# First token parts made from the loads in single steps, first casts shared with Pool, forget gate moved behind the third pair

## The chip, the cores and the metric

The kernel runs on one core of one Trainium2 chip. The metric is the device time of one execution in microseconds (us). Before the change it is 517.13 us, the median of 3 runs (516.63 to 520.16). Five engines work side by side, each through its own queue in order: TensorE (matmuls, transposes), VectorE, ScalarE, Pool (GpSimd) and SP, which here only issues DMAs. The profile calls them PE (its weight loads PEld), DVE, ACT, POOL and SP.

## What is computed

Two residual layers over 512 tokens of 1024 channels, everything in float32. Cut to what matters here, the first layer is:

```python
h = rms_norm(x, norm_g)
proj = h @ w_in
fox_qkv, f_logit, moba_qkv, gate = split(proj)          # 8 fox heads, 8 moba heads of 64
logf = log_sigmoid(f_logit + b_f)                       # one forget value per token and fox head
c = cumsum(logf)                                        # over tokens
logits = q @ k * scale + c[query] - c[key]              # fox: causal, biased by c
out_a = softmax(logits) @ v
out_b = moba(qb, kb, vb)                                # rotary, selected key blocks
x = x + (concat(out_a, out_b) * silu(gate)) @ w_out
```

The second layer is a GLU, a causal depthwise convolution of width 31, a layer norm and an output projection.

## The kernel before

A float32 product is made of three products of rounded parts: each operand is split into `hi` (rounded) and `lo` (the rest), and `hi*hi + hi*lo + lo*hi` is summed. So each block of weights (a chunk of 256 or 260 columns, 1024 rows, 1 MB) is loaded into `wst`, cast to `whi` by ScalarE (L237) and subtracted to `wlo` by VectorE or Pool (L241), in four pieces of 512 columns per partition. Two `wst` buffers let one chunk load while another is split.

**The start.** The tokens arrive transposed, `xt`, in four tiles of 128 tokens (8 channel blocks of 128 each, `fetch_xt`, L279). SP issues in this order: the first `xt` tile in two halves, the first weight chunk in four quarters, the other three `xt` tiles whole, then the untransposed `xs` tiles and the next chunk (L316 to L324). For each tile and half tile, VectorE multiplies by the norm's gain into `hn` (L409), ScalarE casts `hn` to `hhi` (L411), VectorE subtracts to `hlo` (L412). The first chunk's split stands behind the first tile's parts: ScalarE casts all four pieces, Pool subtracts the first and the third, VectorE the others. TensorE begins with 22 matmuls on zeros (`WARM`, L394) and then multiplies tile by tile, 24 matmuls for each (`tok_mm`, L442); for the first chunk all eight `hi*hi` come first, then eight `lo*hi`, then eight with `wlo`. The norm's own factor `rinv` per token comes from ScalarE's squares of `xs` (L419) and a power on Pool (L422), and is applied when a product is read out of PSUM (`qk_chunk`: L468, L470). The second chunk's split (ScalarE, VectorE) is queued behind the first two of these reads.

**The middle.** 16 chunks of projections (`dense`) are interleaved on TensorE with 8 pairs of attention heads (`attention`): pairs 0 to 3 are `moba`, 4 to 7 `fox`. A pair's tile (`tile_of`, L585) is two score matmuls (L590, L592) into one of two `s` banks, a VectorE step that adds the mask or bias and takes the row minimum (`p`, `nm`, L602), ScalarE's exponential (L603), transposes on TensorE into one of two `tp` banks (L606), and a copy out of that bank to `pt`, by ScalarE (L614) and VectorE (L616) in turn. `stacks` (L554) makes a pair's `q`, `k` and `kl` (L570 to L581). L683 multiplies with the values; the result is scaled by `rb`, which comes back from a DMA through `sdram` (L626, L629).

**The forget gate.** The seventh chunk holds the gate's 8 columns. When its last tile is read, `forget` (L513) runs: two VectorE steps on 32 columns, an exponential (L519), twelve more small VectorE steps (a series for the logarithm), a triangle of ones `tri` (an iota on Pool, a comparison on VectorE, L534), four matmuls in eight passes for the cumulative sum (L537), a copy `ct` and a DMA to `cdram` (L541). The fox pairs load their bias rows `cb` from there (L662), and Pool adds the mask to each (L598).

Beside this, Pool splits the weights of the last layer into DRAM (`presplit`, L712): a load by SP, a cast (L718), a subtraction (L719), two DMA issues (L721), for 16 parts.

**What sets the order.** `ORDER` (L79) holds, for each engine, the whole order of this part's instructions, written out as indices into the program; `+n` are steps of `presplit`. Every queue follows it to the letter, so a step that waits holds up everything behind it on its engine.

Of the kernel before, what the change touches and what calls it, by code (L numbers as in the profile page):

```python
# [66 lines left out]
def XLO(t, nc):  # L67
# [22 lines left out]
        694 857-858 788-789 779-782 859-868 721-722 869 817-818 749-750 870-877 851-852 878-880  # L90
        893-906 785-787 890 907-912 790-792 891 913-916 920-937 917 938-939 819-821 944-945 853-855
        822 918 856 940-941 847-850 942-943 948-956 972 881 973 892 1080-1081 957-966 882-888 919
        889 967-968 946-947 969 1085-1086 1114-1115 970-971 976-985 974-975 986-988 1082-1084
        989-990 1144-1145 991-1004 1087 1005 1088 1006 1089 1007-1023 1116-1119 1024-1034 1146-1149
        1035-1044 1072-1075 1174 1045-1056 1175-1182 1057-1071 1090-1113 1120-1143 1150-1173
        1189-1198 1076-1079 1199-1212 1219-1236 1183 1237-1242 1184 1248-1271 1213 1243-1244
        1277-1286 1301 1214 1302-1304 1185-1188 1287-1300 1313-1318 1272-1273 1319-1320 1309-1310
        1321-1322 1215-1218 1323-1328 1245-1247 1329-1335 1337-1338 1336 1344-1346 1305-1307
        1341-1342 1308 1347-1351 1274 1311 1275 1312 1276 1352-1356 1368-1369 1357-1367 1371-1384
        1339-1340 1385-1393 1404 1394 1343 1405 1410-1425 1370 1426-1429 1434 1430-1433 1464-1465  # L100
        1440 1395 1441-1443 1522 1435 1523-1525 1444-1445 1396-1403 1406-1409 1446-1451 1493-1494
        1530-1531 1436-1439 1452-1462 1466-1468 1463 1469-1476 1558-1559 1477 1586-1587 1478-1480
        1495-1497 1481-1482 1532-1533 1483-1492 1498 1613-1614 1499-1506 1560-1561 1507-1508 1588
        1509-1513 1526-1529 1514-1521 1534-1537 1615-1616 1538-1548 1625 1549-1551 1626 1552-1555
        1617-1622 1655 1623-1624 1719 1656 1720-1722 1556-1557 1685-1686 1627-1630 1562-1578
        1690-1691 1579-1580 1657-1660 1581-1584 1727-1728 1585 1687-1689 1723-1726 1589-1592
        1731-1732 1593-1595 1692-1694 1596-1599 1735-1736 1600-1612 1729-1730 1631-1632 1738-1739
        1633-1636 1733-1734 1750-1751 1637-1646 1737 1647-1648 1756-1757 1649-1653 1740 1654
        1661-1664 1762-1763 1665-1668 1741 1669-1673 1767-1768 1674-1675 1742-1747 1772-1773
        1748-1749 1752-1753 1758-1761 1754-1755 1676 1776-1777 1677-1684 1695-1705 1780-1781 1764  # L110
        1769 1783-1784 1770 1765 1771 1766 1706-1718 1774-1775 1778-1779 1782 1785-1797""",
    "DVE": """0 2 12 35-38 1 3 13 15 4-11 14 16-17 19 21 18 20 23 25 22 27 24 29 26 31 28 32 30 43-44
        39-42 33-34 45-47 49 51 50 52-53 48 54 65-66 83-84 55-56 58 85 59 89 57 92-94 96-98 60 95 99
        61-62 100 63 67 70 101 68 102 74 64 111-112 71 75 77 103 69 78 72 76 73 82 79 86 88 80 104
        122-123 90 124-125 105 108 87 109 126 113 91 106 114 81 107 110 118 129 119 121 115 130 137
# [41 lines left out]
WARM2 = 2  # L157
# [7 lines left out]
def tile_kernel(ctx: ExitStack, tc: tile.TileContext, x, xt, w, small0, small1, l1_norm, out):  # L165
# [59 lines left out]
    def split_w(w, ring, eng, parts, cast, swap):  # L225
# [559 lines left out]
    for tl in range(64):  # L785
        with tc.high_priority(HP):
            next(att)
# [522 lines left out]
```

## Time and profile before

| | |
|---|---|
| median of 3 runs | 517.13 us |
| the profiled execution | 519.09 us, of it 517.3 the span that the profile covers |
| busy in the span | TensorE 97%, VectorE 73%, ScalarE 62%, Pool 54% |
| granted TensorE clock, mean | 0.997 of full speed |
| DMA moved | 87.46 MB, mean 169 GB/s |

Times in the profile count from the span's start. A row of a timeline gives the start, the time from the first instruction's start to the last one's end, engine, line, operation, output and inputs, shapes and count, and in brackets the engine's idle time ahead with what ended it. Instructions of an engine overlap a little, so `x4` of 0.62 us can take 2.19 us in all. A DMA's row is its issue alone. A view of stretches gives each engine's busy time in a window, then the granted clock, the mean busy share of the 16 DMA engines and GB/s.

### The profile page before, as it was taken

How to read it: one execution, taken by the hardware profiler on the slowest of the kernel's cores; microseconds unless marked ns; L12 is line 12 of the kernel's file. 1: busy time of each engine (PE TensorE's matmuls, PEld its weight loads, DVE VectorE, ACT ScalarE, POOL GpSimd, SP SyncE). 2: the span in 40 equal slices, each digit the busy share in tenths (PEclk: the TensorE clock that was granted, in tenths of full speed). 3: DMA queues.
4: the chain of work that ended last, by engine and by line, in shares of the span. 5: the costliest groups of instructions: out<-in, count | busy, mean ns of one | idle time of the engine just before them, and what ended most of it. 6: DMA issues, size and time to landing. Idle time of an engine off the chain costs nothing.

```text
span 517.3 us, 9873 instructions
## 1 busy us (share of the span) xinstructions
PE 503.3 (97%) x3694; PEld 460.1 (89%) x3694; DVE 377.4 (73%) x790; ACT 322.3 (62%) x665; POOL 281.7 (54%) x315
## 2 busy tenths in 40 slices
PE   8999999997999999999999999999999999989997
PEld 4999998985889998878779999999999988868997
DVE  6744677779565677767688144999999999897741
ACT  5945678775545787556575723988878656567330
POOL 4265858277598454311402011787999997876200
PEclk9999999999999999999999999999999999989999
DMA  8842244657645450323207698588999947741111
GB/s 287 328 145 72 96 142 164 205 186 236 213 167 178 146 163 26 125 96 123 102 2 293 205 208 241 178 210 208 291 255 236 331 167 264 182 124 41 41 43 42
DMA packets 20856, 87.46 MB, mean 169 GB/s; under 512 B 2692, under 2 KB 5056, under 8 KB 13512
## 3 DMA queue, kind: packets, MB, share of 16 engines
q1 hardware_dynamic: 15512, 59.47, 32.3%
q0 software_dynamic: 5152, 27.27, 20.3%
q8 instruction: 29, 0.48, 0.4%
q14 instruction: 19, 0.16, 0.1%
q10 hardware_dynamic: 144, 0.09, 0.1%
HBM read 57.41 MB, written 10.53 MB: 131 GB/s over the span
## 4 chain that ended last, share of the span: by engine, by line
PE 82%; DVE 7%; DMA 4%; POOL 2%; issue 2%; ACT 2%; SPq 1%; POOLq 0%; ACTq 0%; DVEq 0%
PE mm L442 29%; PE mm L451 8%; PE mm L452 8%; PE mm L453 8%; PE st L442 4%; PE tp L606 3%; PE o L683 3%; PE st L451 2%; PE st L453 2%; PE st L452 2%; PE o L442 2%; PE s L590 2%; PE s L592 2%; POOL pacc L898 2%; DMA xt<-in_xt_dram 1%
## 5 line engine op out<-in xcount | busy, mean ns | idle before, releaser
L898 POOL TENSOR_TENSOR pacc<-pacc,tm 128x256 f32<-128x256 f32 (+1 forms) x129 | 125.2, 981 | 19.7 <-ACT tm L897 12.5
L888 DVE SCALAR_TENSOR_TENSOR s<-u,parts,s 128x256 f32<-128x256 f32 (+1 forms) x207 | 105.9, 566 | 0.7
L442 PE MATMUL mm<-whi,hhi 128*128 128x256 f32 (+1 forms) x352 | 99.0, 288 | 0.6 <-ACT whi L237 0.6
L442 PE MATMUL mm<-wlo,hhi 128*128 128x256 f32 (+1 forms) x352 | 98.7, 287 | 0.5 <-DVE wlo L241 0.4
L442 PE MATMUL mm<-whi,hlo 128*128 128x256 f32 (+1 forms) x352 | 98.3, 286 | 0.0
L897 ACT ACTIVATE tm<-u,parts 128x256 f32<-128x256 f32 (+1 forms) x129 | 69.0, 577 | 15.2 <-POOL pacc L898 14.8
L442 PEld LDWEIGHTS mm<-whi,hhi 128*128 128x128 f32 x352 | 65.8, 189 | 1.8 <-ACT whi L237 1.2
L442 PEld LDWEIGHTS mm<-wlo,hhi 128*128 128x128 f32 x352 | 65.8, 190 | 1.7 <-DVE wlo L241 0.6
L442 PEld LDWEIGHTS mm<-whi,hlo 128*128 128x128 f32 x352 | 65.8, 190 | 0.2
L237 ACT ACTIVATE whi<-wst 128x512 fp32r<-128x512 f32 (+2 forms) x77 | 49.4, 708 | 7.8 <-DMA wst<-in_w_dram 4.1
L603 ACT ACTIVATE p<-p,nm 128x128 f32<-128x128 f32 (+3 forms) x64 | 35.7, 559 | 26.1 <-DVE nm L602 24.2
L241 DVE TENSOR_TENSOR wlo<-wst,whi 128x512 fp32r<-128x512 f32 (+1 forms) x50 | 40.9, 848 | 10.5 <-ACT whi L237 10.3
L241 POOL TENSOR_TENSOR wlo<-wst,whi 128x512 fp32r<-128x512 f32 (+1 forms) x22 | 30.6, 1400 | 28.2 <-ACT whi L237 28.2
L598 POOL TENSOR_TENSOR cb<-cb,mask 128x128 f32<-128x128 f32 x32 | 16.9, 534 | 50.7 <-DVE nm L602 37.4
L451 PE MATMUL mm<-nhi,wx 128*128 128x256 f32 (+1 forms) x104 | 32.6, 313 | 0.0
L452 PE MATMUL mm<-nlo,whi 128*128 128x256 f32 (+1 forms) x104 | 31.9, 308 | 0.0
L452 PE MATMUL mm<-nlo,wx 128*128 128x256 f32 (+1 forms) x104 | 31.8, 306 | 0.0
L453 PE MATMUL mm<-nhi,wx 128*128 128x256 f32 (+1 forms) x104 | 31.8, 306 | 0.0
L453 PE MATMUL mm<-nhi,wlo 128*128 128x256 f32 (+1 forms) x104 | 31.8, 306 | 0.0
L451 PE MATMUL mm<-nhi,whi 128*128 128x256 f32 (+1 forms) x104 | 31.7, 307 | 0.0
L606 PE MATMUL tp<-identf,p 128*128 128x128 f32 x160 | 28.3, 274 | 0.4 <-ACT pt L614 0.3
L477 POOL TENSOR_TENSOR rq<-vq,mhalf 128x16 f32<-128x16 f32 x8 | 25.9, 3240 | 3.4 <-DVE vq L475 3.1
(295 smaller groups left out, 1475.1 us busy)
## 6 DMA issues: line engine op xcount, KB each, us to landing
wst<-in_w_dram SPq DMA_DIRECT2D x29, 1024.0 KB, 5.2
wx<-wst POOLq DMA_DIRECT2D x9, 1024.0 KB, 7.0
wlo<-wst POOLq DMA_DIRECT2D x7, 1024.0 KB, 9.3
pre<-ot POOLq DMA_DIRECT2D x26, 256.0 KB, 3.3
wx<-pre SPq DMA_DIRECT2D x4, 1024.0 KB, 5.2
ot<-in_w_dram SPq DMA_DIRECT2D x13, 256.0 KB, 5.6
wst<-in_w_dram SPq DMA_DIRECT2D x2, 1040.0 KB, 7.2
xs<-in_x_dram SPq DMA_DIRECT2D x4, 512.0 KB, 11.4
```

The source lines that it names most:

```text
L237: A.activation(hi[:, ks], st[:, ks], AF.Copy)
L241: (V if eng is G and parts == 4 and (k % 4 > 0) != swap else eng).tensor_tensor(lo[:, ks], st[:, ks], hi[:, ks].bitcast(F32), op=ALU.subtract)
L442: T.matmul(po, a[:, k, ts], b[:, k, :n], start=first and i == 0, stop=last and i == len(prods) - 1)
L451: T.matmul(po, whi[:, k, cs], a, start=k == 0, stop=False)
L452: T.matmul(po, whi[:, k, cs], b, start=False, stop=False)
L453: T.matmul(po, wlo[:, k, cs], a, start=False, stop=k == KC - 1)
L477: G.tensor_tensor(r, v, mhalf[:, :16].rearrange("p (t h) -> p t h", t=NT), op=ALU.pow)
L603: A.activation(p[:, :w], p[:, :w], AF.Exp, bias=nm, scale=-1.0, accum_out=sm[:, h, t:t + 1])
L606: T.transpose(tp[:, j * P:(j + 1) * P], p[:, j * P:(j + 1) * P], identf)
L888: V.scalar_tensor_tensor(acc[:, o], v, w, first[0][:, :n] if i == 1 else acc[:, o], op0=ALU.mult, op1=ALU.add)
L897: A.activation(tm[:, :n], v, AF.Copy, scale=w)
L898: G.tensor_tensor(pacc[:, o], pacc[:, o], tm[:, :n], op=ALU.add)
```

## The change

- The first `xt` tile is loaded whole, the first weight chunk in two halves.
- `hn` is gone. For each of the eight channel blocks of a tile, ScalarE makes `hhi` straight from `xt` with the gain as its scale, and VectorE makes `hlo` as `xt * gain - hhi` in one step. 8 casts and 8 subtractions of 512 columns become 32 and 32 of 128.
- Of the first chunk's casts, ScalarE does the first and third piece, Pool (`tensor_copy`) the second and fourth. All four subtractions are VectorE's. In Pool's order the two casts and two of the four `rinv` powers now stand ahead of the rope tables (L351, L355).
- `forget` is called after tile 26 of the attention (`FT`), inside the fourth pair. Its 14 small VectorE steps stand together, behind the two score reads that ran at 132.69 and 132.97 us before, and ahead of the tile copy of 136.14 (L616); its exponential on ScalarE behind the tile copy of 137.15 (L614); its matmuls on TensorE ahead of a product that ran at 145.55. `tri` is made on Pool (a memset and a select) in the buffer of tag `e`, behind the eleventh part of `presplit` and ahead of the weight subtraction of 140.33. On VectorE the product with `rb` of 115.84 (L688) moves behind a tile copy and a weight subtraction.
- On SP the gate's DMA stands behind a weight load, the two loads of the first `cb` behind the fourth pair's `sdram` and `rb`; on Pool the first two mask additions, which ran at 146.29, behind the weight subtraction of 161.05.
- TensorE's order is otherwise the same.

The diff without the lists of `ORDER`:

```diff
...
@@ -149,6 +148,7 @@
 L34 = (35,)
 POS7 = 0
 SP3 = 23
+FT = 26
 GLO = ()
 KO = 4
 KORD = (6, 0, 1, 2, 4, 5, 7, 3)
@@ -222,7 +222,13 @@
             SY.dma_start(st[:, k:k + m, :].rearrange("p k n -> p (k n)"), w_ap(off, n, k, m))
         return st, n
 
-    def split_w(w, ring, eng, parts, cast, swap):
+    def low_eng(i, j, eng, parts):
+
+        if eng is not G or parts != 4:
+            return eng
+        return V if i == 0 or (j % 2 == 1) != (i == V1) else G
+
+    def split_w(i, w, ring, eng, parts, cast):
         st, n = w
         if ring == "main":
             hi, lo = flat(main, F32R, "whi", n, 2), flat(main, F32R, "wlo", n, 2)
@@ -231,14 +237,17 @@
         m = KC // parts
         if cast:
             G.dma_start(hi, st)
-        for k in range(0, KC, m):
+        for j, k in enumerate(range(0, KC, m)):
             ks = slice(k, k + m)
-            if not cast:
+            if i == 0 and j % 2:
+                G.tensor_copy(hi[:, ks], st[:, ks])
+            elif not cast:
                 A.activation(hi[:, ks], st[:, ks], AF.Copy)
             if eng is None:
                 A.activation(lo[:, ks], st[:, ks], AF.Copy, scale=-1.0)
             else:
-                (V if eng is G and parts == 4 and (k % 4 > 0) != swap else eng).tensor_tensor(lo[:, ks], st[:, ks], hi[:, ks].bitcast(F32), op=ALU.subtract)
+                low_eng(i, j, eng, parts).tensor_tensor(lo[:, ks], st[:, ks], hi[:, ks].bitcast(F32),
+                                                        op=ALU.subtract)
         if eng is None:
             G.dma_start(lo.bitcast(F32), st, accum_op=ALU.add)
         return hi, lo
@@ -290,7 +299,7 @@
 
     def fetch(i):
         if i < len(wsrc) and i not in PRE:
-            raw[i] = load_w(*wsrc[i], 4 if i == 0 else 1)
+            raw[i] = load_w(*wsrc[i], 2 if i == 0 else 1)
 
     pre = {i: dram.tile([2, P, KC * WC], F32, name=f"pre{i}") for i in PRE}
 
@@ -311,9 +320,9 @@
         if i in PRE:
             wts[i] = load_parts(i)
         elif i < len(wsrc):
-            wts[i] = split_w(raw.pop(i), rings[i], SPLIT_ENG(i, nc), APARTS if i in DMAS else 4 if i == 0 or 17 <= i < 24 else WPARTS, i in CAST, i == V1)
-
-    fetch_xt(0, 2)
+            wts[i] = split_w(i, raw.pop(i), rings[i], SPLIT_ENG(i, nc), APARTS if i in DMAS else 4 if i == 0 or 17 <= i < 24 else WPARTS, i in CAST)
+
+    fetch_xt(0, 1)
     fetch(0)
     for t in range(1, NT):
         fetch_xt(t, 1)
@@ -402,15 +411,12 @@
     rbc = at.tile([P, S], F32, name="rbc")
     hp = {}
     for t in range(NT):
-        hn = v0[:, (t % 2) * KC * P:(t % 2 + 1) * KC * P].rearrange("p (k t) -> p k t", k=KC)
         ts = slice(t * P, (t + 1) * P)
-        for h in range(2):
-            ks = slice(h * 4, h * 4 + 4)
-            V.tensor_tensor(hn[:, ks], xts[t][:, ks], gcol[:, ks, None].to_broadcast([P, 4, P]),
-                            op=ALU.mult)
-            hp[2 * t + h] = hpart = A.activation(hhi[:, ks, ts], hn[:, ks], AF.Copy)
-            V.tensor_tensor(hlo[:, ks, ts], hn[:, ks], hhi[:, ks, ts].bitcast(F32),
-                            op=ALU.subtract)
+        for k in range(KC):
+            g = gcol[:, k:k + 1]
+            hp[2 * t + k // 4] = hpart = A.activation(hhi[:, k, ts], xts[t][:, k], AF.Copy, scale=g)
+            V.scalar_tensor_tensor(hlo[:, k, ts], xts[t][:, k], g, hhi[:, k, ts].bitcast(F32),
+                                   op0=ALU.mult, op1=ALU.subtract)
         if t == 0:
             with tc.issue_after(hpart.ins):
                 split(0)
@@ -503,8 +509,6 @@
             A.activation(vt[grp][:, t, c0:c0 + m], po[:, :m], AF.Copy, scale=rinv[:, t:t + 1])
             if m < n:
                 V.tensor_scalar(zf[:, t, :], po[:, m:n], rinv[:, t:t + 1], None, op0=ALU.mult)
-            if t == NT - 1 and n > m:
-                forget()
             yield
 
 
@@ -530,8 +534,10 @@
         V.scalar_tensor_tensor(h, h, 1.0, s, op0=ALU.add, op1=ALU.mult)
         V.scalar_tensor_tensor(lf, z, 0.0, h, op0=ALU.min, op1=ALU.add)
 
-        tri = at.tile([P, S], F32, tag="p", name="tri", bufs=PB)
-        V.tensor_scalar(tri, distance(S), 0.0, None, op0=ALU.is_ge)
+        tri = at.tile([P, S], F32, tag="e", name="tri", bufs=1)
+        G.memset(tri, 1.0)
+        G.affine_select(out=tri, in_=tri, compare_op=ALU.is_ge, fill=0.0, base=0, pattern=[[1, S]],
+                        channel_multiplier=-1)
         pc = bank("o", 1)
         for t in range(NT):
             T.matmul(pc[:NH, t * P:S], lf[:, t, :], tri[:, :S - t * P], start=t == 0,
@@ -785,6 +791,8 @@
     for tl in range(64):
         with tc.high_priority(HP):
             next(att)
+        if tl == FT:
+            forget()
         total = max(total, done) + PACE[tl // 16]
         advance(int(total))
     with tc.high_priority(HP):
```

## Rows read from the trace of the kernel before

**Rows 1.** the page, part 1: busy time, share of the span, instructions

```profile
PE 503.3 (97%) x3694; PEld 460.1 (89%) x3694; DVE 377.4 (73%) x790; ACT 322.3 (62%) x665; POOL 281.7 (54%) x315
```

**Rows 2.** timeline of TensorE, 0 to 13 us: start us, us, engine, line, operation, idle before

```profile
1.44 6.78 PE L394 MATMUL mm<-idle 128*128 128x512 bf16 x22 [1.44 <-DVE idle L391]
...
12.90 0.28 PE L442 MATMUL mm<-whi,hhi 128*128 128x256 f32 x1
```

**Rows 3.** timeline of all engines, 0 to 50 us

```profile
18.45 0.48 ACT L468 ACTIVATE qk<-mm,rinv 128x256 f32<-128x256 f32 x1 [0.35 <-POOL rinv L422]
...
20.02 2.19 ACT L237 ACTIVATE whi<-wst 128x512 fp32r<-128x512 f32 x4
...
20.68 2.50 DVE L241 TENSOR_TENSOR wlo<-wst,whi 128x512 fp32r<-128x512 f32 x4
...
21.79 0.40 PE L442 MATMUL mm<-whi,hhi 128*128 128x256 f32 x2
...
22.10 1.05 ACT L419 ACTIVATE xs<-xs 128x1024 f32<-128x1024 f32 x1
```

**Rows 4.** stretches: length, then busy us of each engine, clock, DMA share, GB/s

```profile
116.40:129.30 12.90, 9.68 (x66) 7.51 (x66) 12.03 (x30) 6.77 (x18) 9.24 (x13) 1.00 0.78 236
```

**Rows 5.** waits, 110 to 146 us: us in total, times, longest

```profile
PE s L590 <- DVE nm L602: 2.4, 2, 1.9
...
PE s L592 <- DVE kl L581: 0.9, 2, 0.7
```

**Rows 6.** timeline of VectorE, 104 to 140 us, the gate's steps

```profile
111.90 1.24 DVE L515 TENSOR_TENSOR fz<-zf,parts 128x32 f32<-128x32 f32 x1
...
117.38 1.27 DVE L523 TENSOR_SCALAR fu<-fe 128x32 f32<-128x32 f32 x1
...
125.28 0.40 DVE L529 SCALAR_TENSOR_TENSOR fh<-fh,fq 128x32 f32<-128x32 f32 x2
```

**Rows 7.** chain of waits, 450 to 475 us: start, us, what

```profile
470.63 1.20 ACT tm L897 x3
```

**Rows 8.** ScalarE's groups by form, 0 to 320 us: busy, mean ns

```profile
L603 ACT ACTIVATE p<-p,nm 128x256 f32<-128x256 f32 x16 | 8.0, 502 | 3.7 <-DVE nm L602 3.6
...
L603 ACT ACTIVATE p<-p,nm 128x128 f32<-128x128 f32 x16 | 6.4, 400 | 6.0 <-DVE nm L602 4.3 <-DVE fh L530 1.3
```

**Rows 9.** timeline of Pool, 104 to 172 us

```profile
116.98 1.62 POOL L719 TENSOR_TENSOR ot<-ot 128x512 f32<-128x512 f32 x1
...
129.28 0.61 POOL L718 CAST ot<-ot 128x512 fp32r<-128x512 f32 x1 [3.40 <-DMA ot<-in_w_dram]
...
133.02 1.28 POOL L719 TENSOR_TENSOR ot<-ot 128x512 f32<-128x512 f32 x1
...
140.33 1.31 POOL L241 TENSOR_TENSOR wlo<-wst,whi 128x520 fp32r<-128x520 f32 x1 [4.98 <-ACT whi L237]
```

**Rows 10.** timeline of all engines, 0 to 50 us, second token tile

```profile
10.61 1.29 DVE L409 TENSOR_TENSOR v<-xt,parts 128x512 f32<-128x512 f32 x2 [1.26 <-DMA xt<-in_xt_dram]
```

**Rows 11.** stretches as in rows 4, at the start

```profile
4.00:6.00 2.00, 2.00 (x8) 0.82 (x7) 1.75 (x9) 0.87 (x2) 1.80 (x4) 1.00 0.82 210
...
6.00:8.00 2.00, 2.00 (x12) 0.95 (x9) 1.54 (x6) 1.03 (x3) 1.68 (x4) 1.00 0.94 308
...
8.00:10.00 2.00, 1.45 (x7) 0.81 (x6) 0.69 (x1) 1.89 (x3) 1.29 (x2) 1.00 1.03 411
```

**Rows 12.** timeline of TensorE, 116 to 131 us, the gate's matmuls

```profile
127.73 2.32 PE L537 MATMUL o<-tri,lf 128*8 128x512 f32 x8
```

**Rows 13.** timeline of VectorE, 104 to 200 us

```profile
136.14 0.29 DVE L616 COPY pt<-tp 128x128 f32<-128x128 f32 x1 [2.62 <-PE tp L606]
...
170.62 0.68 DVE L602 CUSTOM_DVE_ANT_0 p<-s,cb 128x512 f32<-128x512 f32 x1
```

**Rows 14.** timeline of ScalarE, 104 to 140 us

```profile
137.15 0.39 ACT L614 ACTIVATE pt<-tp 128x256 f32<-128x256 f32 x1 [2.83 <-PE tp L606]
```

**Rows 15.** timeline of TensorE, 133 to 141 us

```profile
139.31 0.38 PE L606 MATMUL tp<-identf,p 128*128 128x128 f32 x2
```

More of the change, by code (lines that the diff above doesn't have):

```diff
@@ L95 @@
[L95 to L106, printed above, removed]
@@ new lines @@
+        822 914 852 936-939 948-956 972 877 973 888 1080-1081 957-966 878-884 915 885 967-968
+        942-943 969 1085-1086 1114-1115 970-971 976-985 974-975 986-988 1082-1084 989-990 1144-1145
+        991-1004 1087 1005 1088 1006 1089 1007-1023 1116-1119 944-947 1024-1034 1146-1149 1035-1044
+        1072-1075 1174 1045-1056 1175-1182 1057-1071 1090-1113 1120-1143 1150-1173 1189-1198
+        1076-1079 1199-1212 1219-1236 1183 1237-1242 1184 1248-1271 1213 1243-1244 1277-1286 1301
+        1214 1302-1304 1185-1188 1287-1300 1313-1318 1272-1273 1319-1320 1309-1310 1321-1322
@@ new lines @@
+        1526-1529 1514-1521 1534-1537 1615-1616 1538-1548 1625 1549-1551 1626 1552-1555 1617-1622
+        1655 1623-1624 1719 1656 1720-1722 1556-1557 1685-1686 1627-1630 1562-1578 1690-1691
+        1579-1580 1657-1660 1581-1584 1727-1728 1585 1687-1689 1723-1726 1589-1592 1731-1732
+        1593-1595 1692-1694 1596-1599 1735-1736 1600-1612 1729-1730 1631-1632 1738-1739 1633-1636
+        1733-1734 1750-1751 1637-1646 1737 1647-1648 1756-1757 1649-1653 1740 1654 1661-1664
+        1762-1763 1665-1668 1741 1669-1673 1767-1768 1674-1675 1742-1747 1772-1773 1748-1749
@@ new lines @@
+        1752-1753 1758-1761 1754-1755 1676 1776-1777 1677-1684 1695-1705 1780-1781 1764 1769
+        1783-1784 1770 1765 1771 1766 1706-1718 1774-1775 1778-1779 1782 1785-1797""",
+    "DVE": """0 2 12 53-56 1 3 13-40 4-11 49 41-48 50 61-62 57-60 51-52 63-65 67 69 68 70-71 66 72 83-84
+        101-102 73-74 76 103 77 107 75 110-112 114-116 78 113 117 79-80 118 81 85 88 119 86 120 92
+        82 129-130 89 93 95 121 87 96 90 94 91 100 97 104 106 98 122 140-141 108 142-143 123 126 105
+        127 144 131 109 124 132 99 125 128 136 147 137 139 133 148 155 134 145 149 152 138 157 153
+        160 156 146 161 135 150 162 158 154 165 151 166-167 170 159 169 163 189 203 171-184 168 204
+        208 190 186-187 191 209 192 164 205 193 188 194 185 210-211 199 195 200 196-197 206-207 212
+        198 201 216-219 213 202 220 222 214 221 226 223 227 230 225 215 234 236 231 237 232 238 224
+        239 242 240 228 233 235 241 247 229 244 243 245 248-249 254 265-266 261 269 250-252 246 255
+        274 256 278 257-258 262 253 259 285 260 332 275 267 263 286 270 287 271 268 264 289 292 272
+        303 298 288 334 273 304 299 293 307 276 279-282 308 300 305 310 277 306 283 311 284 309 338
+        315-316 312 290 318 294 313 295 291 319 340 321 317 322 296-297 314 336 330 324 320 325
+        327-328 301 323 326 302 331 342 333 335 337 339 341 343 329 344-345""",
@@ L141 @@
+    "POOL": """0 2 1 9-12 3-8 13-14 20 15 21 16-19 27-30 22-26 36 31 37 32-35 43 38 44 39-42 +24 45-46 +20
+        47-48 50 49 51 +8 53 52 54-56 +8 57-59 +2 61-63 +2 60 64-65 67-69 72-73 66 74-76 70-71 79-88
+        77-78 89-92""",
+    "SP": """0-15 19-21 +3 25 16-18 26 +3 22-24 +3 31 +2 27-29 +2 32 30 33-37 +2 38-39 +1 43-45 40-42 51
+        46 52 48 47 49-50 53 57-58 54-56""",
 }
```

58 lines of the change are left out of this document (19 added, 39 removed).

## The prediction

> **What bounds the kernel now.** I read the page first, then TensorE's stretches, the waits, and the timelines of the two places that the change touches. TensorE is busy for 503.3 of 517.3 us [rows 1], so the other engines matter where they make it wait, and a gain made early stays: what follows is TensorE's own queue, whose order the change leaves as it was but for four matmuls. Two places lose time. At the start the first real matmul cannot begin before the 22 warming matmuls are through (about 7.85 us), and the first token tile's 24 products last until 12.9 [rows 2], where 24 at the later pitch would take 2.9 (two in 0.40 us [rows 3], one in 0.28 [rows 2], so 0.12 each). In the stretch 116.4 to 129.3 TensorE is busy for 9.7 of 12.9 us [rows 4]. The waits of that stretch name the reader of scores (`nm`, L602) and `kl` (L581), both on VectorE: 2.4 + 0.9 = 3.3 us [rows 5]. What delays them is the forget gate, which stands between them in VectorE's queue: the addition of the bias took 1.24 us for 32 columns, the first step after the exponential 1.27, while two later steps took 0.40 together [rows 6].
>
> **Part one, the start.** Removed: eight VectorE multiplications `hn`, eight ScalarE casts of 512 columns, two of ScalarE's weight casts, two Pool subtractions and three load issues. Added: 32 ScalarE casts and 32 VectorE steps of 128 columns, two casts on Pool, two weight subtractions on VectorE.
>
> ScalarE's new cast has a scale per partition. The nearest row with one is the convolution's tap, 256 columns each 0.40 us in a run of three [rows 7]. The exponential's rows show what half the columns save: 502 against 400 ns [rows 8], 0.10 us. That makes 0.30; taking off 128 columns at the plain cast's 1 ns (four of 512 in 2.19 us [rows 3]) makes 0.27. I take 0.30, since the exponential is the nearest in size: 8 x 0.30 = 2.4 us a tile, where two plain casts took 1.1. VectorE's step lies between 0.20 us (32 columns [rows 6]) and 0.62 (512 columns, four in 2.50 [rows 3]), by its columns near 0.28, 2.3 us a tile; it now comes behind the cast, and VectorE keeps pace. So VectorE's multiplication leaves the path and ScalarE becomes its owner.
>
> First tile: the first cast waits for the whole of `xt` instead of its half. But TensorE's warming covers everything to 7.85 us, and the first two of four weight pieces should then be ready, on ScalarE and Pool side by side (Pool's cast 0.61 us [rows 9], ScalarE's 0.55); before, all four came one after another on ScalarE. The tile ends sooner than 12.9, and with 24 x 0.12 behind 7.85 not before 10.7.
>
> That lead has to pass ScalarE. From the landing of the second `xt` tile (10.6 us in the kernel before [rows 10]) to the second chunk's first low part ScalarE now does, in its written order, 24 casts (7.2 us), two squares (1.05 each, 2.1), four reads of products (20.02 - 18.45 = 1.6) and one weight cast (0.55), then VectorE one subtraction (2.50/4 = 0.62) [rows 3]: 12.1 us. With the landing as before this is at 22.7, and TensorE wanted the part two matmuls behind 21.79 [rows 3], at 22.03: 0.65 us late. So the start gains the time by which that load lands sooner, less 0.65.
>
> How much sooner? The loads move in rows of 2 KB per partition until the weights are in and of 4 KB after. That the half MB of this tile took 1.3 us at the last rate below puts the 1.5 MB ahead of it from about 2 to 9.3 us. The queues' throughput was 210 GB/s at 4 to 6 us, 308 at 6 to 8 and 411 from 8 on [rows 11]; per busy share 256, 328 and 399. If larger rows cost what the later ones did, the 1.5 MB take 18% less (328 against 399), 1.3 us; I take 1.3. The lower end is 0 (the slow stretch is not the rows' size); the upper 2.6, the slowest stretch's 256 for all of it. Start: gain 1.3 - 0.65 = 0.65 us; ends -0.65 and +1.95, and with casts of 0.27 (24 x 0.03 = 0.7 more) 2.4, where TensorE's own work ends it: 96 x 0.12 behind 7.85 is 19.4, against 21.79. Below nothing is possible, since ScalarE's added work is certain and the landing is not. The rope products on Pool, now behind two of the `rinv`, have no reader before the end of the first chunk's four tiles, and nothing but them is queued behind Pool's two casts while these wait for loads; they cost nothing.
>
> **Part two, the forget gate.** Removed from VectorE's queue before 130 us: 14 small steps, `tri` and `ct`; from Pool the iota. With them the 3.3 us of waits should go, and the eight passes of its matmuls (127.73 to about 130.0, 2.25 us [rows 12]) move some 16 us down TensorE's queue. TensorE reaches what followed them 3.3 + 2.25 = 5.5 us sooner, and pays 2.25 back when it gets to them.
>
> The 14 steps now stand together in VectorE's queue, behind two score reads and ahead of the `pt` copy that began at 136.14 after 2.6 idle us [rows 13]. The gap is not free: after two steps comes the exponential, and it stands in ScalarE's queue behind the `pt` copy at 137.15 [rows 14], which waits for TensorE. That ends at 137.54 - 5.5 = 132.0; the exponential makes it 132.2. Twelve dependent steps at 0.20 (two in 0.40 [rows 6]) end at 134.6 at the best. Queued behind them is the `pt` copy, and behind that the score reads. TensorE's transposes of 139.31 [rows 15] use one of two banks, and theirs is freed by that copy; TensorE is there at 133.8. With E the chain's end and 0.4 for the copy, it waits E + 0.4 - 133.8. At E = 134.6 that is 1.2 us, so the move gains 2.1; even at E = 136.7.
>
> Pool splits the last layer's weights then: cast, subtraction, two issues, over and over, and its times hang on loads, not on TensorE [rows 9]. The rows of the gate show what this does: the step of 1.27 us ended at 118.65, Pool's subtraction of 116.98 at 118.60 [rows 9]. The one of 133.02 ends at 134.30 [rows 9]. If one or two steps slip in before it and ten follow it, E = 136.3; Pool should be some 0.3 us sooner, freed of the same collisions, so I take 136.0: a wait of 2.6, a gain of 0.7. The Trainium skill, "SBUF - State Buffer", section "Who interferes with whom", says that a VectorE operation with two inputs in SBUF, or in its two-port mode, is held for the whole of a Pool operation that reads SBUF. The trace agrees (1.24 and 1.27 against 0.20 us); without that rule the sum would have E = 134.6, with it 136.0 or later.
>
> At nothing: `tri`, made by Pool in two operations behind its split, sits where Pool was idle for 5.0 us before 140.33 [rows 9]; without that cover its 1 us would delay a weight part. The gate's DMA goes behind a weight load on SP, with `sdram` and `rb` queued behind it, whose VectorE step also comes after the gate's copy `ct`; the bias loads follow those; the first mask addition goes behind the next weight parts, but the first reader of a bias came only at 170.62 [rows 13], 40 us after the gate's matmuls had ended.
>
> **The sum.** 0.65 + 0.7 = 1.35 us. Against the profiled execution's own 519.09 us (span 517.3, the rest around it) that is 517.7; the median of the runs is 517.13, so I forecast 515.8.
>
> **Rivals.**
> 1. *Gate hidden.* Pool waits for its loads just then (it did for 3.4 us before 129.28 [rows 9]), E = 134.6, gain 2.1 + 0.65 = 2.75: 514.4. For it: Pool's idle gaps; against: its next two casts fall right there.
> 2. *The wait comes back larger.* Both split rounds fall inside the chain: 2 x (0.61 + 1.29) + 12 x 0.20 on top of 132.2 is E = 138.4, a wait of 5.0, a loss of 1.7 less the 0.65: slower, 518.2. It decides from E = 136.7 on (with the start's gain, 137.4). For it: Pool's work is not moved with TensorE's; against: its rounds are 3 us apart, and the chain alone lasts 2.4. The rule of the Trainium skill just named is what would make it so.
> 3. *The loads do not come sooner.* Then ScalarE's casts cost 0.65 and the gate gives 0.7: 517.1, no change. For it: the slowest stretch had a busy share of 0.82 [rows 11], so not every byte waited for a row; against: both steeper stretches move 4 KB rows.
>
> **How the numbers follow.** Forecast 0.40, rival 1 0.20, rival 2 0.12, rival 3 0.15; 0.13 are left for what I did not see. About 1% (5.2 us) is what a measurement of this kernel tells from no change. All four lie inside it: same 0.87. Beyond it on the fast side needs both upper ends and no new wait (2.4 + 3.3 = 5.7): 0.07; on the slow side a wait over 3.3 + 5.2 us, more than the whole chain takes between Pool's rounds: 0.06. Range: from the first upper ends (1.95 + 2.1 = 4.05: 513.1) to rival 2 with a late load (518.2 + 1.3, of which I keep 0.3): 513.1 to 518.5; the forecast's own is 514.8 to 516.8.
>
> **What would show it.** Right: `xt` casts of about 0.30 us pitch, ScalarE without idle time from the second `xt` tile to the second chunk's weights; no waits for `nm` and `kl` of a `moba` pair near 115 to 124 us; a new wait of TensorE for a tile copy (`pt`, L616) of some 2.6 us near 134, with the gate's steps lying between Pool's. Wrong: second `xt` tile landing no sooner than 10.6, or the second chunk starting after 21.8; a new wait over 3.7 us; or none, with the exponential issued early. The forecast fails most likely by E, which hangs on Pool's phase.

## The result, and the profile after

| | kernel before | changed kernel |
|---|---|---|
| median of 19 runs each, us | 517.88 (515.75 to 522.02) | 514.45 (512.93 to 516.17) |
| the profiled execution's own time, us | 519.09 | 513.34 |
| its span, us | 517.3 | 511.6 |

The ratio is 0.9932, 95% interval [0.9914, 0.9949]: 3.4 us less, between 2.6 and 4.5. That lies inside the 1% that the forecast took for no change, on its fast side; the forecast was 515.8, a gain of 1.35. So the direction was right and the gain two and a half times as large. One thing has to be known for all times here: near 460 us the granted clock falls to the lower of its two levels (1.2 instead of 2.4 GHz) for some 3.4 us in some executions of every kernel and not in others, which moves an execution by some 2 us, and the profiled execution of before had that fall while the one of the changed kernel had not. In executions without it (a mean granted clock of 0.999 or more) the medians are 516.48 us (26 of the kernel before, all from the experiments below) and 513.48 (14 of the changed kernel), 3.0 us apart.

TensorE's order is the same in both kernels but for the gate's four products, so each of its instructions can be matched with the same one of the other timeline. The lead of the changed kernel (start before minus start after) is the best instrument of this case:

| instruction of TensorE | before, us | after, us | lead, us |
|---|---|---|---|
| second token tile, first product | 12.90 | 11.60 | 1.30 |
| first chunk, last eight low products | 19.87 | 18.91 | 0.96 |
| second chunk, first product | 21.79 | 21.18 | 0.61 |
| second chunk, first low product | 22.03 | 21.91 | 0.12 |
| second chunk, fourth product | 22.15 | 22.13 | 0.02 |
| score product behind the first `kl` wait | 119.64 | 118.71 | 0.93 |
| behind the first `nm` wait | 123.16 | 121.55 | 1.61 |
| behind the second `nm` wait | 125.94 | 122.15 | 3.79 |
| behind the second `kl` wait | 127.06 | 122.82 | 4.24 |
| first product past the gate's old place | 129.98 | 123.37 | 6.61 |
| first product past the gate's new place | 145.55 | 141.27 | 4.28 |
| before the clock falls in the one trace | 462.78 | 458.83 | 3.95 |
| after it | 466.04 | 460.60 | 5.44 |

From 22 to 118 us the lead stays at 0.0. It all comes from the gate: four waits are worth 4.2 us, the gate's products are passed 2.4 us sooner and paid for 2.3 us later; small waits behind 144 us take 0.3 back. This one pair of profiles shows some 0.9 us more than the medians without the fall; why is not shown. The last 1.5 us are the clock of the profiled execution of before, not the change.

Busy time, on the page of the changed kernel (part 1), answers to [rows 1]: TensorE does 1.9 us less busy time, in a span 5.7 us shorter.

```profile
PE 501.4 (98%) x3694; PEld 458.5 (90%) x3694; DVE 376.3 (74%) x807; ACT 325.1 (64%) x687; POOL 278.5 (54%) x316
```

The stretches of the changed kernel (length, then busy us of PE, PEld, DVE, ACT, POOL, the clock, the DMA share, GB/s) answer to [rows 4, 11]:

```profile
4.00:6.00 2.00, 2.00 (x8) 0.83 (x7) 0.67 (x4) 0.88 (x3) 0.00 (x0) 1.00 0.99 329
6.00:8.00 2.00, 2.00 (x11) 0.78 (x8) 2.00 (x7) 2.00 (x7) 0.67 (x1) 1.00 1.03 416
8.00:10.00 2.00, 1.99 (x13) 1.49 (x12) 2.00 (x4) 1.31 (x4) 1.11 (x1) 1.00 1.02 416
116.40:129.30 12.90, 12.90 (x103) 11.40 (x102) 8.11 (x27) 8.76 (x26) 7.55 (x11) 1.00 0.83 258
```

The loads run at 329 and 416 GB/s where they ran at 210 and 308, and TensorE is busy for all of the 12.9 us in which it had been busy for 9.7.

The start, on ScalarE's timeline (start, us, engine, line, operation, idle before) of the changed kernel, answers to [rows 3, 10]:

```profile
5.12 2.45 ACT L417 ACTIVATE hhi<-xt,parts 128x128 fp32r<-128x128 f32 x8 [2.39 <-DMA parts<-in_small_dram]
...
9.41 4.80 ACT L417 ACTIVATE hhi<-xt,parts 128x128 fp32r<-128x128 f32 x16 [0.62 <-DMA xt<-in_xt_dram]
14.12 1.04 ACT L425 ACTIVATE xs<-xs 128x1024 f32<-128x1024 f32 x1
...
18.90 0.46 ACT L476 ACTIVATE sqs<-mm,rinv 128x256 f32<-128x256 f32 x1
19.77 0.47 ACT L474 ACTIVATE qk<-mm,rinv 128x256 f32<-128x256 f32 x1 [0.41 <-POOL rinv L428]
...
20.50 2.19 ACT L245 ACTIVATE whi<-wst 128x512 fp32r<-128x512 f32 x4
```

on VectorE's, with the steps that the input of the second `rinv` (`vv`) stands behind:

```profile
17.79 1.23 DVE L418 SCALAR_TENSOR_TENSOR hlo<-xt,parts,hhi 128x128 fp32r<-128x128 f32 x4 [0.92 <-ACT hhi L417]
...
18.94 0.15 DVE L427 TENSOR_SCALAR vv<-ssx 128x1 f32<-128x1 f32 x1
```

and on TensorE's, where two small waits, for ScalarE's cast of 20.50 and for VectorE's subtraction behind it, end the lead:

```profile
11.60 1.12 PE L448 MATMUL mm<-whi,hhi 128*128 128x256 f32 x8
...
21.18 0.50 PE L448 MATMUL mm<-whi,hhi 128*128 128x256 f32 x2 [0.19 <-ACT whi L245]
21.91 0.39 PE L448 MATMUL mm<-wlo,hhi 128*128 128x256 f32 x1 [0.22 <-DVE wlo L249]
```

The gate in its new place, on ScalarE's, VectorE's and Pool's timelines, answers to [rows 6, 9, 13, 14]:

```profile
128.12 0.21 ACT L523 ACTIVATE fe<-fna 128x32 f32<-128x32 f32 x1
130.45 0.39 ACT L620 ACTIVATE pt<-tp 128x256 f32<-128x256 f32 x1 [2.12 <-PE tp L612]
```

```profile
128.36 0.18 DVE L527 TENSOR_SCALAR fu<-fe 128x32 f32<-128x32 f32 x1 [0.64 <-ACT fe L523]
...
131.18 1.16 DVE L534 SCALAR_TENSOR_TENSOR fh<-fh,fs 128x32 f32<-128x32 f32 x1
132.37 0.19 DVE L535 SCALAR_TENSOR_TENSOR lf<-fz,fh 128x32 f32<-128x32 f32 x1
132.48 0.28 DVE L622 COPY pt<-tp 128x128 f32<-128x128 f32 x1
```

```profile
130.26 0.61 POOL L724 CAST ot<-ot 128x512 fp32r<-128x512 f32 x1 [6.14 <-DMA ot<-in_w_dram]
130.95 1.34 POOL L725 TENSOR_TENSOR ot<-ot 128x512 f32<-128x512 f32 x1
```

The exponential runs at 128.12, ahead of the `pt` copy of 130.45. The chain starts at 128.36, its last step at 132.37, and the copy behind it at 132.48. TensorE meets no wait; its transposes that use the freed bank come just behind, and the gate's products find `lf` 6 us old and `tri` (Pool's select at 136.96, 0.61 us) 1.4 us old:

```profile
133.19 0.49 PE L612 MATMUL tp<-identf,p 128*128 128x128 f32 x3
...
139.02 2.32 PE L543 MATMUL o<-tri,lf 128*8 128x512 f32 x8
```

### The profile page after: what moved, and what is told of

Same layout as the page of the kernel before. It is cut to its first block, busy times and chain, and to the rows that moved or that the text cites. A ratio compares the mean times of both kernels' runs of the same rounds, so it can differ in the third digit from the quotient of the medians.

```text
span 511.6 us, 9911 instructions
## 1 busy us (share of the span) xinstructions
PE 501.4 (98%) x3694; PEld 458.5 (90%) x3694; DVE 376.3 (74%) x807; ACT 325.1 (64%) x687; POOL 278.5 (54%) x316
## 4 chain that ended last, share of the span: by engine, by line
PE 78%; DVE 6%; POOL 5%; DMA 5%; ACT 3%; issue 2%; SPq 0%; POOLq 0%; ACTq 0%
PE mm L448 27%; PE mm L457 8%; PE mm L458 8%; PE mm L459 8%; PE st L448 4%; PE o L689 3%; PE tp L612 3%; PE st L457 2%; PE st L459 2%; PE st L458 2%; PE o L448 2%; PE s L596 2%; POOL pacc L906 2%; PE s L598 2%; DMA pre<-ot 2%
## 5 line engine op out<-in xcount | busy, mean ns | idle before, releaser
L245 ACT ACTIVATE whi<-wst 128x512 fp32r<-128x512 f32 (+2 forms) x75 | 48.1, 710 | 5.0 <-PE mm L448 2.5
L249 DVE TENSOR_TENSOR wlo<-wst,whi 128x512 fp32r<-128x512 f32 (+1 forms) x52 | 43.4, 868 | 10.0 <-ACT whi L245 9.6
L249 POOL TENSOR_TENSOR wlo<-wst,whi 128x512 fp32r<-128x512 f32 (+1 forms) x20 | 28.8, 1452 | 20.0 <-ACT whi L245 20.0
```

Of the source, the lines that this page charges most:

```text
L249: low_eng(i, j, eng, parts).tensor_tensor(lo[:, ks], st[:, ks], hi[:, ks].bitcast(F32), op=ALU.subtract)
```

## The experiments

Ratios are to the kernel before in the same job, with their 95% intervals; leads are those of TensorE, matched as above.

**Each part alone.** `gate_only` is the kernel before with the gate's lines, its `tri` by Pool and every queue place that belongs to them, and with the loads, `hn` and the casts of before; `start_only` is its complement. `gate_only` against the kernel before:

```
-            if t == NT - 1 and n > m:
-                forget()
...
+        if tl == FT:
+            forget()
```

> The kernel before with the forget gate moved behind the third pair and nothing of the new start. Theory A (the gate pays nearly all, the start's lead dies on ScalarE): TensorE runs as in the kernel before up to 118 us, gains 4.2 to 4.3 us at the two stacks and score reads, and the time lies within 1 us of the changed kernel, 513.6 to 515.4 us. Rival B (the move is worth the 0.7 us forecast, the rest of the 3.4 us is the start's): 516.5 to 517.5 us, and TensorE's lead behind the gate's matmuls is under 1.5 us.

Measured: 514.53 us, ratio 0.9945 [0.9924, 0.9966]. TensorE leads the kernel before by 4.06 us behind the waits, by 3.79 behind the gate's products and by 3.70 at the end. Theory A holds.

> The changed kernel with the forget gate put back in its old place; the new start stays. Theory A: TensorE leads by 1.3 us at the second token tile and by nothing from about 22 us on; the waits of 3.3 us for nm and kl are there again; the time is that of the kernel before, 517.4 to 518.4 us. Rival B: the start keeps 1 us or more of its lead behind 22 us, and the time is 514.9 to 516.9 us.

Measured: 517.40 us, ratio 0.9994 [0.9974, 1.0015]. The lead is 1.23 at the second token tile, 0.09 at 22 us and none from 23 us until the gate. There it becomes 0.78, since TensorE's waits in the old place are smaller in this execution than in [rows 5] (stretch 110 to 130 us: us in total, times, longest):

```profile
PE s L597 <- DVE nm L609: 1.8, 2, 1.3
PE s L599 <- DVE kl L588: 0.5, 2, 0.4
```

So the start's lead does not reach the gate (beside `gate_only`, whose own start is 0.17 us behind that of the kernel before, the changed kernel keeps 0.2). What the gate cost in its old place was 2.3 us here and 3.3 in the other profile. Whether the execution or the new start made these waits smaller is not shown: the four executions of `start_only` without the clock's fall have a median of 515.89 us, the eleven of the kernel before in the same job 516.46.

**The exponential's place.** The list of ScalarE's order has the gate's exponential one place ahead of the copy. `exp_behind` turns the two round, as the forecast had read them:

```
-        160-161 166 150 168 176-177 162-163 165 171 180-181 178 169 182 185 183-184 179 190 209 187
-        186 211 188-189 191-194 217 210 195-196 220 197-198 218 203 199-200 204 201-202 212-216 219
+        160-161 166 150 168 176-177 162-163 165 171 180-181 178 169 182 185 183-184 179 190 209 186
+        187 211 188-189 191-194 217 210 195-196 220 197-198 218 203 199-200 204 201-202 212-216 219
```

Here 187 is the exponential and 186 the copy.

> The changed kernel with the gate's exponential behind the copy of the transposed tile (pt, L620) on ScalarE, where the forecast had it, instead of ahead of it. Theory A (the chain's end E counts, and it was early only since the exponential went ahead): the exponential goes from 128.12 to about 130.85, the chain ends at 135.0 to 136.5 instead of 132.5, TensorE waits 2.3 to 3.8 us for the VectorE copy at the transposes of 132.61, and the time rises by 2 to 4 us: 516.5 to 518.5 us. Rival D (the chain has slack, other work of TensorE fills the wait): TensorE waits under 1 us there and the time is 514.2 to 515.4 us.

Measured: 517.81 us, ratio 0.9995 [0.9974, 1.0015]: by the medians the whole gain is gone. ScalarE's, VectorE's and TensorE's timelines of that kernel:

```profile
130.73 0.22 ACT L523 ACTIVATE fe<-fna 128x32 f32<-128x32 f32 x1
...
130.98 0.26 DVE L527 TENSOR_SCALAR fu<-fe 128x32 f32<-128x32 f32 x1 [3.25 <-ACT fe L523]
...
132.33 2.61 DVE L533 SCALAR_TENSOR_TENSOR fh<-fh,fq 128x32 f32<-128x32 f32 x5
...
135.31 0.28 DVE L622 COPY pt<-tp 128x128 f32<-128x128 f32 x1
...
135.65 0.55 PE L612 MATMUL tp<-identf,p 128*128 128x128 f32 x3 [2.30 <-DVE pt L622]
...
142.04 2.31 PE L543 MATMUL o<-tri,lf 128*8 128x512 f32 x8 [0.45 <-DVE ot L694]
```

The copy comes 2.83 us later than in the changed kernel, the transposes 2.46 later; with 0.55 more at the gate's own products, whose bank is freed by a VectorE product (L694) that is late as well, TensorE is 3.0 us behind the changed kernel. Theory A holds, and with it the forecast's mechanism: a chain that ends at 135.3 costs a wait of 2.3 us.

**What is queued behind the chain.** Is it the copy alone? In `exp_behind_copy_early` the exponential is late again, but the copy stands ahead of the step that waits for it. `copy_mid` moves the copy in the changed kernel into the middle of the chain.

In VectorE's list 171 to 184 are the gate's steps and 168 is the copy; the first added line is that of `exp_behind_copy_early` (beside the edit above), the second that of `copy_mid`:

```
-        160 156 146 161 135 150 162 158 154 165 151 166-167 170 159 169 163 189 203 171-184 168 204
+        160 156 146 161 135 150 162 158 154 165 151 166-167 170 159 169 163 189 203 171-172 168 173-184 204
...
+        160 156 146 161 135 150 162 158 154 165 151 166-167 170 159 169 163 189 203 171-177 168 178-184 204
```

> The exponential behind the copy on ScalarE as in the slowed run, and on VectorE the copy of the transposed tile ahead of the step that waits for the exponential. The chain ends as late as there, at 135 to 136 us. Theory A (TensorE waits for the copy and for nothing else of what is behind the chain): the wait of 2.3 us for pt is gone, the score reads come 2.5 us later and cost at most 1 us, 514.0 to 515.5 us. Rival E (everything behind the chain counts): the same 2 to 3 us are lost at the next transposes, for p, and the time is 516.2 us or more.

Measured: 517.43 us, ratio 0.9973 [0.9948, 0.9998]. The copy runs at 129.37 and TensorE passes the transposes without a wait, to stop half a microsecond further on:

```profile
137.02 0.50 PE L596 MATMUL s<-k,q 128*128 128x512 f32 x1 [3.16 <-DVE nm L608]
```

Rival E is right in size, though TensorE stops at the next score product and not at the transposes: the score read behind the copy frees the bank of the next score product. TensorE starts it 0.62 us after that read starts (136.40 to 137.02), so with the product at 133.76 the read is due at 133.14; the copy is due at 133.19 - 0.34 = 132.85. Two due times within 0.3 us of each other, and the changed kernel met both by 0.4 us (copy 132.48, read 132.68). In this profile the granted clock fell at 138 us, behind the wait, and not near 460; the wait does not come from it, and the four executions without a fall took 516.05 to 516.60 us.

> The changed kernel itself, as it is, beside the next three on one chip. Both theories: 513.5 us in executions whose granted clock stays up near 459 us, 515.7 us in those where it falls there. Theory A (Pool's rounds hang on loads and move from execution to execution): Pool's first round near the gate need not start at 130.26 us as in the other profile; where it starts at 129 us or earlier, the chain ends at 133 us or later and TensorE waits 0.3 to 1 us for the copy. Rival D: chain and rounds lie as in the first profile, within 0.2 us.

Measured: 513.72 us, ratio 0.9904 [0.9872, 0.9936]. Pool's first round starts at 130.00, the copy at 132.46, there is no wait: rival D, for this pair of executions.

> The changed kernel with one thing moved: the VectorE copy of the transposed tile from behind the gate's 14 steps to behind the seventh of them. Theory A: no wait of TensorE for pt near 133 us, 0 to 1 us faster than the changed kernel in the same job, since only some of its executions wait. Rival E: the score reads are next in line, TensorE waits as long a little later, the time is the changed kernel's.

Measured: 515.11 us, ratio 0.9919 [0.9886, 0.9952], with the clock's fall in more of its executions; its TensorE lies within 0.3 us of the changed kernel's from the start to 459 us, where its clock falls. No gain: there was no wait to take away, and the read behind the copy is due at nearly the same time.

**The loads and ScalarE.** `small_loads` gives the changed kernel the old pieces (below); `gate_loads` gives `gate_only` the new pieces, by the reverse of this edit, and nothing else of the start (SP's list has the loads renumbered).

```
-            raw[i] = load_w(*wsrc[i], 2 if i == 0 else 1)
+            raw[i] = load_w(*wsrc[i], 4 if i == 0 else 1)
...
-    fetch_xt(0, 1)
+    fetch_xt(0, 2)
```

> The changed kernel with the first loads in the old pieces (xt in two, the first weights in four). Theory A, the forecast's own sum: the second xt tile lands at about 10.6 instead of 9.4, ScalarE's chain of 12.1 us goes on from there, TensorE gets the second chunk's first low part 1.0 to 1.3 us later than in the changed kernel (23.0), and the time rises by as much: 515.4 to 515.9 us. Rival F (the loads' pieces change nothing): the second tile lands within 0.4 us of 9.4 and the time is 514.2 to 514.8 us.

Measured: 515.36 us, ratio 0.9960 [0.9937, 0.9982]. ScalarE's second tile starts at 10.33 instead of 9.41, and TensorE's second chunk is late by as much:

```profile
10.33 4.80 ACT L417 ACTIVATE hhi<-xt,parts 128x128 fp32r<-128x128 f32 x16 [1.32 <-DMA xt<-in_xt_dram]
...
22.82 0.39 PE L448 MATMUL mm<-wlo,hhi 128*128 128x256 f32 x1 [0.22 <-DVE wlo L249]
```

22.82 - 21.91 = 0.91 for a landing 0.92 later, and TensorE keeps that delay (0.91) to 133 us. Theory A holds for the start: landing to second chunk is one chain, and the pieces are worth 0.9 us of it. At the gate, with a round of Pool's at 127.67, the copy comes at 134.05: the delay becomes 1.25 there, 1.75 at the gate's products, and 1.44 at the end, about what the two ratios differ by (0.9960 and 0.9932 of 518 us).

> The kernel before with the gate moved and with the larger first loads alone: xt in one piece, the first weights in two; the products hn, the casts of 512 columns and the split of the weights are those of the kernel before. Theory A (ScalarE's 32 casts of 0.30 us eat what the loads bring): the second xt tile lands near 9.4 instead of 10.6 us and, without those casts, TensorE enters the second chunk 0.6 to 1.0 us sooner than with the old loads (21.8 to 22.0): 513.6 to 514.0 us. Rival F (the loads bring nothing that lasts: the second chunk waits for its own weights or for the reads of products): 514.3 to 514.8 us, the second chunk at 21.7 or later.

Measured: 515.61 us, ratio 0.9949 [0.9929, 0.9969], TensorE's first low product of the second chunk at 22.55 (22.20 in `gate_only`). Without the new casts the sooner load brings nothing, as rival F has it, but neither by its wait nor in its time: TensorE enters the second chunk without a wait, 0.35 us late since 13.09, where it had waited 1.24 us for one of VectorE's weight subtractions (0.86 in `gate_only`). VectorE's pair of `hn` products then started at 10.05 but took 2.38 us instead of 1.29 [rows 10], while Pool subtracted (7.89 to 11.29). Another 1.0 us goes at the gate, with waits of 0.56 us for `pt` and 0.45 at the gate's products.

**ScalarE's order at the second chunk.** If ScalarE is the owner, its order should move the second chunk. `weights_first` puts the four casts of the second chunk's weights (40 to 43 in ScalarE's list) ahead of the second read of products (46 and 47), `one_first` only the first of them; on VectorE the subtractions 57 to 60 and the sum 62 are turned round in the same way. The first added line is that of `weights_first`, the second that of `one_first`:

```
-    "ACT": """0-27 36 28-31 37 32-35 44-47 40-43 38-39 48-59 77 81 60-61 91 73-76 94 98-101 62-64 102-103
+    "ACT": """0-27 36 28-31 37 32-35 44-45 40-43 46-47 38-39 48-59 77 81 60-61 91 73-76 94 98-101 62-64 102-103
...
+    "ACT": """0-27 36 28-31 37 32-35 44-45 40 46-47 41-43 38-39 48-59 77 81 60-61 91 73-76 94 98-101 62-64 102-103
```

`one_first_copy_mid` and `both_again` are `one_first` with the edit of `copy_mid`.

> The changed kernel with two lists turned round: the four casts of the second chunk's weights stand on ScalarE ahead of the second read of products (qk and sqs of the second token tile), and VectorE's four subtractions ahead of the sum of that read. Theory A (ScalarE's order, not the loads, holds the second chunk back): its first cast goes from 20.50 to about 19.3 us, the first low part is ready near 20.5, TensorE enters the second chunk at its own end of the first, about 21.0, and is 0.8 to 1.0 us ahead of the changed kernel from there to the end: 513.4 to 513.7 us. Rival C (the second chunk's weights land late, or the later readers give the lead back by 118 us): 514.2 to 514.8 us, with TensorE level with the changed kernel at 118 us.

Measured: 514.82 us, ratio 0.9950 [0.9932, 0.9968]. The cast does go to 19.32, and a new wait takes over:

```profile
20.89 0.28 PE L448 MATMUL mm<-whi,hhi 128*128 128x256 f32 x1
22.28 0.39 PE L448 MATMUL mm<-whi,hhi 128*128 128x256 f32 x1 [1.11 <-ACT sqs L476]
```

Neither theory named it: the second chunk takes two token tiles in turn, so its second product needs the bank that the delayed read frees. TensorE stays 0.5 us behind the changed kernel to 133 us and then waits 0.83 us for `pt`, with a round of Pool's at 128.51 in the chain.

> The changed kernel with only the first of the four casts of the second chunk's weights ahead of the second read of products on ScalarE (and its subtraction ahead of that read's sum on VectorE). With all four ahead, TensorE waited 1.11 us for that read, since the second chunk takes two token tiles in turn and needs both banks. Theory A (the order on ScalarE holds the second chunk back, in both ways): first cast 19.3, read of the second tile over at 20.65, first low part near 20.6, TensorE enters the second chunk at 20.95 without a wait and is 0.7 to 0.9 us ahead of the changed kernel at 22 us and at 118 us. Rival C (later readers or loads give the lead back): less than 0.3 us ahead at 118 us. The time is 513.5 to 513.8 us under A, if the end of the gate's chain does not move; each Pool round that slides into the chain adds about 1 us.

Measured: 513.47 us, ratio 0.9916 [0.9887, 0.9946]. TensorE's first low product is at 21.05, 0.86 sooner than in the changed kernel, and it is still 0.6 ahead at 133 us. There this execution loses it: Pool's round starts at 127.45, the chain ends with a copy at 133.30, TensorE waits 0.9 us and, with 0.46 more at the gate's products, leaves the stretch 0.7 us behind the changed kernel:

```profile
133.64 0.55 PE L612 MATMUL tp<-identf,p 128*128 128x128 f32 x3 [0.92 <-DVE pt L622]
```

Theory A for the start, and its proviso for the gate.

> As the last, and on VectorE the copy of the transposed tile (pt, L622) goes from behind the gate's 14 steps to the middle of them, behind the seventh. Theory A (the copy behind the chain is what TensorE waits for, and Pool's rounds lengthen the chain in some executions): no wait of TensorE for pt near 133 us wherever the chain ends, also at 134 us or later; 513.2 to 513.8 us, and 0 to 1 us faster than the last one. Rival E (the score reads behind the chain are next in line): a wait for p or nm of about the same size comes 2 to 3 us later, and the time is that of the last one.

Measured: 514.38 us, ratio 0.9920 [0.9891, 0.9949]. The median misses theory A's range and lies above that of `one_first`; four of the six executions had the clock's fall. In the profiled one there is no wait for `pt`, and TensorE is 0.66 us ahead of the changed kernel up to the gate and 0.99 at the end (span 510.6). That this comes from the copy's new place is not shown: Pool's two rounds left a gap in this execution (127.04 to 129.0 and from 130.54), and the chain ended 1.9 us sooner than in `one_first`.

> The kernel with the first cast of the second chunk's weights moved up and the copy in the middle of the chain, once more, beside the changed kernel on one chip. Theory A: the 0.8 us of the start last to the end and no wait for pt: 0.8 to 1.5 us faster than the changed kernel, 512.4 and 514.6 us in the two kinds of execution. Rival C: under 0.4 us faster.

Measured: 512.78 us, ratio 0.9897 [0.9860, 0.9933], beside 513.72 of the changed kernel in the same job. TensorE is 0.80 us ahead of that one at 21 us, 0.61 up to the gate and 1.03 at the end. Theory A. This is the kernel of `one_first_copy_mid` once more, whose median was 514.38, and the intervals of the ratios overlap with the changed kernel's. What shows the gain is the matched timelines, and the executions without the clock's fall: its six took 512.34 to 512.83 us, the fourteen of the changed kernel 512.93 to 514.93. It keeps on ScalarE the time that the larger loads had won.

## Why the forecast was right in direction and short in size

**What bounds the kernel.** Right: the waits of [rows 5] were the gate's and went with it, and TensorE's own queue carried the lead to the end.

**The start, 0.65 us.** The prices were right: eight casts in 2.45 us and sixteen in 4.80 (0.30 each), VectorE's steps 0.27 (16 in 4.28), the first tile ending at 11.6. The landing was 1.2 us sooner than in [rows 10] (1.3 taken; against the old pieces in the same kernel 0.92). The step that failed here is the sum of ScalarE's chain from that landing, 12.1 us; it was 12.36 (9.41 to 21.16 + 0.61). It left out a wait: the second tile's read stood still until 19.77 for `rinv`, which Pool could make only when VectorE had computed its input at 18.94, behind the new steps that follow ScalarE's casts. What was left at TensorE was 0.12 us, and 0.02 a few products later. Of the 0.53 us missing from 0.65, 0.1 is the landing, 0.3 this chain, and 0.14 the time from the end of the subtraction (21.77) to the product (21.91), which the sum put at nothing.

**The gate, 0.7 us.** Two terms were mis-sized and one step was wrong. The waits of 3.3 us were worth 4.2: each wait of TensorE cost 0.2 to 0.3 us more than its idle time on the timeline of before (0.68, 0.51, 1.85 and 0.18 us idle; 0.93, 0.68, 2.18 and 0.45 of lead). Idle time counts from the end of the instruction ahead, but without a wait the next one starts sooner than that. The second of the four, before:

```profile
122.37 0.28 PE L442 MATMUL mm<-whi,hlo 128*128 128x256 f32 x1
123.16 0.36 PE L590 MATMUL s<-k,q 128*128 128x256 f32 x1 [0.51 <-DVE nm L602]
```

In the changed kernel the second of these starts 0.12 us after the first (121.43 and 121.55), here 0.79 after it: 0.67 us lost, 0.51 of them idle. The payback was right (2.25 taken, 2.33 measured). The new wait of 2.6 us was not there, because the exponential does not stand behind the `pt` copy of [rows 14] in ScalarE's list but ahead of it (the section on the change has it behind as well, wrongly): so the chain began at 128.36, not 132.2. This is the step that failed in this part, and the forecast had it among its signs of being wrong: no new wait, with the exponential issued early. `exp_behind` makes the forecast's reading true and comes near its numbers: chain from 130.98 (132.2 taken), copy at 135.3 (136.0 taken), a wait of 2.3 us (2.6 taken). The transposes that wait are those one group behind [rows 15].

**Pool inside the chain.** The forecast took 1.4 us for Pool's rounds, and by the trace they cost about that: without them the twelve steps from 128.36 on, 0.22 us apart with 0.39 for the reciprocal, would have let the copy start at 131.1 instead of 132.48. The step of 1.16 us ends at 132.34, where Pool's subtraction (130.95 and 1.34) ends. The Trainium skill, "SBUF — State Buffer", section "Who interferes with whom", says that a VectorE operation with two SBUF inputs, or in its two-port mode, waits for the whole of a Pool operation that reads SBUF and was issued first. The trace agrees for the two-input steps (1.16 us against 0.19). A step with one input was held as well (1.29 us for 32 columns in `exp_behind_copy_early`, where the same form took 0.18 in the changed kernel, and the 1.27 of [rows 6]); whether it ran in that mode no row shows. Even so the chain was in time, by 0.4 us.

**The rivals.** Rival 1 (gate hidden) came nearest, by another way: Pool did wait for its loads, 6.1 us, but what hid the gate was the early exponential. Rival 2's wait of 5.0 us occurred in no run: both of Pool's rounds lay in the chain in `one_first` and in `weights_first`, with waits of 0.92 and 0.83, and in `exp_behind` it was 2.3. Rival 3 did not occur: the loads came sooner; their gain was spent on ScalarE.

**What was luck.** 514.45 us lies in the stated range, and beside rival 1's 514.4, although both parts of the sum were wrong: in the profiles the gate gave 3.7 to 3.9 us instead of 0.7 and the start 0.0 to 0.2 instead of 0.65.

**Left open.** How often the changed kernel itself waits for the chain: two profiles show none, and its margin is 0.4 us. But four kernels with the same gate lost time there: 0.92 (`one_first`), 0.83 (`weights_first`), 0.56 (`gate_loads`) and about 0.3 us (`small_loads`), each with some 0.45 more at the gate's products. In kernels that differ from it by under 1 us at that point Pool's first round began anywhere from 127.0 to 130.5 us and the chain's end moved with it.

## What to carry to other kernels

Read the place of each moved instruction from the order that is written, on every engine it passes, before anything is costed; one place in one list was here the whole difference between 3.4 us and nothing. When a chain of small steps is moved, list all that is queued behind it and when each is due: taking the first one out only handed the wait to the second here. A transfer made sooner paid here only as far as the engine that turns its data into operands had room: the larger loads were worth 0.9 us, the new casts on ScalarE spent it, and one cast moved in ScalarE's order (`one_first`) brought 0.6 of it back. And count a wait from where the next instruction would have started, not from the end of the one ahead.

## What the runs showed of the hardware

Products of TensorE overlap: one of 256 columns is shown with 0.28 us, and the next starts 0.12 us after it. So the idle time in a profile understates what a wait costs, by 0.17 to 0.33 us in the four waits of the gate, as the leads show.

The granted clock can fall in one execution and not in another that does the same before. The stretches of the changed kernel, and then of `gate_only`:

```profile
440.00:458.00 18.00, 15.78 (x74) 12.25 (x74) 15.58 (x34) 11.10 (x24) 14.02 (x19) 1.00 0.53 142
458.00:462.00 4.00, 4.00 (x37) 4.00 (x36) 3.56 (x9) 3.33 (x10) 2.22 (x3) 1.00 0.37 156
```

```profile
440.00:458.00 18.00, 15.79 (x74) 12.26 (x73) 16.48 (x37) 11.15 (x24) 14.31 (x19) 1.00 0.52 137
458.00:462.00 4.00, 4.00 (x24) 4.00 (x24) 3.10 (x9) 2.45 (x7) 2.42 (x3) 0.60 0.42 176
```

TensorE had been busy for 15.8 of 18 us in both; then one was granted 1.00 and the other 0.60, 24 products instead of 37 in 4 us (full clock is 2.4 GHz; the mean of 0.60 is mostly the lower level, 1.2). In `exp_behind_copy_early` the clock fell at another place, behind the long wait:

```profile
134.00:138.00 4.00, 0.98 (x6) 0.90 (x7) 3.67 (x13) 0.94 (x3) 3.05 (x5) 1.00 0.61 203
138.00:142.00 4.00, 4.00 (x23) 4.00 (x23) 3.02 (x6) 4.00 (x11) 2.90 (x2) 0.57 0.38 118
```

It stayed at 1.00 there in `exp_behind`, where TensorE had been busy for 2.35 of the same 4 us. What decides it is not shown here.
